# One more seven-product group a layer; copies of the weight sums moved to ScalarE; input sums queued behind the last split

## The chip, the cores and the metric

The kernel runs on one core of a Trainium2 chip. A core has TensorE (matmuls; the profile calls it PE, its weight loads PEld), VectorE (DVE), ScalarE (ACT), GpSimd (POOL) and SyncE (SP). Each engine works through its own queue in order. Transfers can be issued from SP, ScalarE and GpSimd, and an issue is one entry in that queue. The metric is the device time of one execution in microseconds; less is better.

## What is computed

A decoder of two layers on one sequence of 512 tokens of width 1024. Cut to what matters here:

```
for l in range(2):
    h = rms_norm(x, norm_mix[l])
    (m_qk, m_v, m_o, m_i, m_f, r_x, r_g, a_q, a_k, a_v, a_qi, a_ki, a_w, gates) = split(h @ w_in[l])
    ... three branches: mLSTM, RG-LRU, sparse attention ...
    x = x + merged @ w_out[l]
    h = rms_norm(x, norm_ffn[l])
    ff_g, ff_u = split(h @ ffn_up[l])                 # 3072 columns each
    ff_g = causal_dwconv(ff_g, ffn_conv_w[l], ffn_conv_b[l])
    x = x + (gelu(ff_g) * ff_u) @ ffn_down[l]
out = rms_norm(x, norm_final)
```

All of it is in float32.

## The kernel before, in words

**Units and splits.** The weights are packed into units of 128 x 1024 floats (512 KB) in the order of their use. SP loads a unit into a `raw` buffer (two of them; during seven-product groups two `quad` buffers more). ScalarE then writes its high part `wh` and VectorE the rest `wl` (`hl_split`, lines 216 and 217), up to three or four units ahead of their use. The inputs are kept the same way as `xh` and `xl`. A product is three matmuls: `wl` with `xh`, `wh` with `xl`, `wh` with `xh`.

**Sections of a layer.** `mv` (line 306), then `sm`, `rx`, `qk`, `qi`, `q`, `k`, `av`, `mo` (lines 262 and 268), with the mLSTM, the recurrence, the index scores and the attention as streams that are advanced between the groups; then the merged branches and the output projection, the second norm, and the feed-forward part in three chunks of eight columns of 128. `rope_pair` sends its results through DRAM with transfers from GpSimd. `k_turn`, `gd` and `g` are steps of the first sections; `g` (line 773) is loaded by GpSimd for the mLSTM. Each norm raises `rs` to the power -0.5 on GpSimd (lines 376 and 399). In layer 0 the rope tables are made on VectorE beside `mv` and `sm`.

**Seven-product groups.** Two feed-forward columns take four plain groups (`f_group`, 24 matmuls of 512 columns each). Pairs that stand in `QUADS` are made by seven products of half the size instead of eight (`quads`, `q_mm`, line 296: 24 matmuls of 256 columns each). Such a group needs sums of input halves (`x_sums`, lines 1030 and 1033: four additions, four differences and four splits, once a layer) and sums of weight units. For each group `u` the weight sums are four DRAM tiles `wsb`, `wsc`, `wse`, `wsg`. Each is a copy of a unit and then an accumulating transfer that adds another unit or another sum: `wse` gets `wsc` added, and `wsg` gets `wse`.

**What sets the order.** The program is traced in one order, and a scheduler with a simulated time line decides in which order each engine's queue gets its entries. `tick` counts slots; at some slots it takes the next step of `g_sums` (line 142). Copies and additions are all issued from GpSimd. Nothing in the program ties them to an instruction of another engine, except that an addition waits for its copy and for the sum that it adds. `tc.issue_after(ins)` (here `after`) queues what it encloses behind `ins` on that instruction's engine; it is an order of issue, not a wait for its end.

Of the kernel before, what the change touches and what calls it, by code (L numbers as in the profile page):

```python
# [15 lines left out]
ALU = mybir.AluOpType  # L16
# [20 lines left out]
NK = 385  # L37


QUADS = {(0, 4), (0, 6)} | {(c, i) for c in (1, 2) for i in (0, 2, 4, 6)}  # L40
SECTIONS = ("mv", "sm", "rx", "qk", "qi", "q", "k", "av", "mo")


# [1 line left out]
def tile_trunk(ctx, tc, x, pos, wts, chan, rgw, const, norm_mix, norm_ffn, norm_final, out, depth=2, dbg=None):  # L45
    nc = tc.nc
    V, A, T, G = nc.vector, nc.scalar, nc.tensor, nc.gpsimd

    def pool(name, bufs, **kw):
        return ctx.enter_context(tc.tile_pool(name=name, bufs=bufs, **kw))  # L50
# [4 lines left out]
    slot = pool("slot", 1)  # L55
# [21 lines left out]
    def S1(tag, shape=(P, 4, 512), dt=F32):  # L77
        return slot.tile(list(shape), dt, tag=tag, name=tag)
# [35 lines left out]
    for l in range(depth):  # L114
        u = l * per
        ffn = u + per - (NH // HC) * 3 * HC
        plan += [(u + i, None) for i in range(ffn - u)]
        u = ffn
        for c in range(NH // HC):
            for g in range(HC // 2):  # L120
                if (c, 2 * g) in QUADS:
                    plan += [(u, o) for o in "abcedfg"]
# [6 lines left out]
    st = dict(dma=0, spl=0, use=0, slot=0)  # L129
    raws, spl, alt, own = {}, {}, {}, {}  # L130
    wsum = {}
# [8 lines left out]
            extra.add(i)  # L140

    def g_sums():
        def put(dst, src, **kw):
            G.dma_start(out=dst, in_=src, max_dma_last_dim=1024, **kw)

        def first_(u):
            w = wsum[u]
            for k, n in (("b", 0), ("c", 1), ("e", 0), ("g", 3)):
                yield put(w[k], wts[u + n])

        def then(u):
            w = wsum[u]
            for k, src in (("b", wts[u + 1]), ("c", wts[u + 2]), ("e", w["c"]), ("g", w["e"])):
                yield put(w[k], src, accum_op=ALU.add)

        gs = list(wsum)
        yield from first_(gs[0])
        for u, v in zip(gs, gs[1:] + [None]):
            f = first_(v) if v is not None else iter(())
            for _ in then(u):  # L160
                yield 1
                yield next(f, None)

    bg = g_sums()

    def held(l):
# [48 lines left out]
    def hl_split(ps, h, l):  # L215
        a = A.activation(out=h, in_=ps, func=AF.Copy)  # L216
        v = V.tensor_tensor(out=l, in0=ps, in1=h.bitcast(F32), op=ALU.subtract)  # L217
        return a, v

    def after(ins):  # L220
        return tc.issue_after(getattr(ins, "ins", ins))
# [2 lines left out]

    def tick():
        st["slot"] += 1
        p = st["slot"] % 308
        if p > 8 and p % (3 if p < 170 else 2 if p < 220 else 4) == 0:
            next(bg, None)

    def pump():
        tick()
        for g in list(streams):
            if g[1]:
                with tc.high_priority():
                    r = next(g[0], None)
            else:
                r = next(g[0], None)
            if r is None:
                streams.remove(g)  # L240
# [47 lines left out]
    def q_mm(ps, x, start=True):  # L288
        tick()
        h, l = [w.rearrange("p (k c) -> p k c", c=2 * P) for w in unit()]  # L290
        for j in (1, 0):
            i = 0
            for k in range(4):
                for a, b in ((l, 0), (h, 1), (h, 0)):
                    i += 1
                    T.matmul(ps[:, j * 256:(j + 1) * 256], lhsT=a[:, k, j * P:(j + 1) * P], rhs=x[b][:, k, :],  # L296
                             start=start and j == 1 and i == 1, stop=j == 0 and i == 12,
                             skip_group_check=True)
# [205 lines left out]
    for l in range(depth):  # L504
        if l == 0:
            res["src"] = x
            nrm = Norm(norm_mix[0:1, :], ("S1", "S2", "S4", "S5"))
# [7 lines left out]
            v = nrm.scaled(0)  # L515
# [7 lines left out]
            with after(st["pair"][0]), after(st["pair"][1]):  # L523
                v = nrm.scaled(1)
# [7 lines left out]
                with after(a1[1]):  # L532
                    v = nrm.scaled(2)
# [3 lines left out]
                    v = nrm.scaled(3)  # L537
# [8 lines left out]
        e = SimpleNamespace()  # L546
# [471 lines left out]
        nrm = Norm(norm_ffn[l:l + 1, :], ("S9", "S6"))  # L1018
# [7 lines left out]
        def x_sums():  # L1026
            qa, qb = [S1(g, (P, 2, 4, 256)) for g in ("S6", "S9")]
            a = [qa[:, 0], qa[:, 1], qb[:, 0], qb[:, 1]]
            for n in (2, 3, 0, 1):
                V.tensor_tensor(out=a[n], in0=xq[n][0].bitcast(F32), in1=xq[n][1].bitcast(F32), op=ALU.add)  # L1030
            for key, g, d, i0, i1, op in (("b", "S1", 3, 2, 3, ALU.subtract), ("c", "S2", 2, 0, 2, ALU.subtract),
                                          ("e", "S3", 0, 3, 0, ALU.subtract), ("f", "S7", 1, 1, 0, ALU.add)):
                V.tensor_tensor(out=a[d], in0=a[i0], in1=a[i1], op=op)
                o = S1(g, (P, 2, 4, 256), dt=FR)
                hl_split(a[d], o[:, 0], o[:, 1])
                xq[key] = (o[:, 0], o[:, 1])
# [41 lines left out]
            for j in range(2):  # L1078
                hidden(i + j, m + j, gt[:, j, :], up[j])

        x_sums()
        nch = NH // HC
        for cidx in range(nch):
            hh = [S1("S4", dt=FR), S1("S6", dt=FR)]
            hl = [S1("S5", dt=FR), S1("S9", dt=FR)]
            i = 0
            while i < HC:
                m = cidx * HC + i
                if (cidx, i) in QUADS:
                    quads(i, m)  # L1090
# [12 lines left out]
            if end:  # L1103
                nrm = Norm(norm_final[0:1, :] if last else norm_mix[l + 1:l + 2, :], ("S1", "S2"))
# [19 lines left out]
def _pack(w_in, w_branch, w_out, ffn_up, ffn_down, depth):  # L1124
# [10 lines left out]
    for l in range(depth):  # L1135
# [41 lines left out]
        for c in range(NH // HC):  # L1177
            for i in range(0, HC, 2):
                m = c * HC + i
                if (c, i) in QUADS:  # L1180
                    for k, o in ((0, 0), (0, DFF), (D // 2, DFF), (D // 2, 0)):
# [82 lines left out]
```

## Time and profile before

| | |
|---|---|
| Median of three runs | 2179.81 us (2177.36 to 2180.73) |
| Profiled execution | 2172.2 us, of which its span is 2170.4 us |
| Busy, share of the span | TensorE 88%, VectorE 58%, ScalarE 40%, GpSimd 10% |
| Software queue of GpSimd's transfers | 127.44 MB, 24.7% of 16 engines |
| Queue of SP's loads | 200.30 MB, 29.2% of 16 engines |
| Chain that ended last | PE 81%, DMA 14%, DVE 3% |

The page cuts the span into 40 slices of 54 us and gives the busy share of each engine in tenths; for the granted TensorE clock and the share of the transfer engines there are rows of the same kind. A group's row gives line, engine, operation, tiles, count, then busy time and mean, then the idle time ahead of it and what ended it. A row of the timeline is start, length, engine, line, operation, tiles, with the idle time ahead of it in square brackets.

### The profile page before, as it was taken

What the parts mean: (1) busy time and instruction counts of PE and PEld (TensorE: products, weight loads), DVE (VectorE), ACT (ScalarE), POOL (GpSimd) and SP (SyncE); (2) the same over time, 40 slices, a digit from 0 to 9 for tenths busy, and PEclk for the clock granted to TensorE, in tenths of its full rate; (3) what the DMA queues carried; (4) which work ended last, traced back from release to release, by engine and by line L of the source; (5) the groups of instructions that cost most, each with busy time, mean ns of one, the idle gap of its engine ahead of it and who ended that gap; (6) DMA issues with size and microseconds to landing.
All of it is one profiled execution on the core that took longest, in us unless ns stands there. A gap on an engine that the chain in (4) does not pass through costs nothing.

```text
span 2170.4 us, 26601 instructions
## 1 busy us (share of the span) xinstructions
PE 1909.3 (88%) x10380; PEld 1627.7 (75%) x10380; DVE 1265.5 (58%) x2131; ACT 863.1 (40%) x1309; POOL 223.1 (10%) x314
## 2 busy tenths in 40 slices
PE   2366006999999999999999999999999999999998
PEld 1244004888888888989899878888888788999896
DVE  1252006786864447647667579777834457667584
ACT  1133004444444235425345466444342334445353
POOL 3433432121000000000000101210000000000000
PEclk6678557999999999999999999999999999999999
DMA  9999999675232332435454325853232233455452
GB/s 324 280 288 283 218 202 233 187 212 144 78 100 93 94 110 94 154 109 185 136 163 145 135 88 154 240 155 93 69 121 87 90 114 126 137 157 165 132 175 82
DMA packets 121758, 333.74 MB, mean 154 GB/s; under 512 B 10904, under 2 KB 52376, under 8 KB 119584
## 3 DMA queue, kind: packets, MB, share of 16 engines
q1 hardware_dynamic: 55584, 200.30, 29.2%
q0 software_dynamic: 64320, 127.44, 24.7%
q10 hardware_dynamic: 1728, 4.31, 0.6%
q8 instruction: 81, 1.33, 0.3%
q14 instruction: 45, 0.37, 0.1%
HBM read 312.06 MB, written 103.30 MB: 191 GB/s over the span
## 4 chain that ended last, share of the span: by engine, by line
PE 81%; DMA 14%; DVE 3%; issue 1%; ACT 1%; POOL 0%; POOLq 0%; ACTq 0%; DVEq 0%
PE A L262 25%; PE A L306 19%; PE A L268 12%; PE s L296 11%; PE t L296 5%; DMA wsc<-in_wts_dram 5%; DMA wsb<-in_wts_dram 5%; PE o L296 2%; DMA wse<-wsc 2%; PE o L836 1%; DMA wse<-in_wts_dram 1%; DMA wsg<-in_wts_dram 1%; PE o L762 1%; PE s L797 1%; PE t L849 1%
## 5 line engine op out<-in xcount | busy, mean ns | idle before, releaser
L262 PE MATMUL A<-xh,wl 128*128 128x512 f32 (+1 forms) x1072 | 428.5, 402 | 158.8 <-DVE wl L217 157.7
L217 DVE TENSOR_TENSOR wl<-raw,wh 128x1024 fp32r<-128x1024 f32 x294 | 358.8, 1222 | 350.2 <-ACT wh L216 348.1
L262 PE MATMUL A<-xl,wh 128*128 128x512 f32 (+1 forms) x1072 | 424.4, 398 | 4.2 <-DVE xl L217 4.2
L216 ACT ACTIVATE wh<-raw 128x1024 fp32r<-128x1024 f32 x294 | 309.8, 1056 | 296.7 <-PE A L306 127.5
L262 PEld LDWEIGHTS A<-xh,wl 128*128 128x128 f32 x1072 | 207.0, 193 | 213.7 <-DVE wl L217 154.8
L268 PE MATMUL A<-xh,wh 128*128 128x512 f32 (+1 forms) x1072 | 275.5, 391 | 0.0
L306 PE MATMUL A<-wh,S 128*128 128x512 f32 x832 | 256.1, 390 | 0.0
L262 PEld LDWEIGHTS A<-xl,wh 128*128 128x128 f32 x1072 | 207.2, 193 | 50.3 <-DVE xl L217 4.9
L268 PEld LDWEIGHTS A<-xh,wh 128*128 128x128 f32 x1072 | 195.5, 188 | 43.0 <-issue 0.5
L306 PEld LDWEIGHTS A<-wh,S 128*128 128x128 f32 x832 | 156.3, 188 | 33.3
L306 PE MATMUL A<-wl,S 128*128 128x512 f32 x416 | 162.6, 394 | 0.0
L296 PE MATMUL s<-S,wh 128*128 128x256 f32 x768 | 138.8, 282 | 0.0
L296 PEld LDWEIGHTS s<-S,wh 128*128 128x128 f32 x768 | 118.8, 190 | 0.2
L296 PE MATMUL s<-S,wl 128*128 128x256 f32 x384 | 108.1, 282 | 0.0
L469 DVE SCALAR_TENSOR_TENSOR m<-A,ch,m 128x511 f32<-128x511 f32 (+2 forms) x88 | 64.8, 744 | 46.1 <-ACT m L465 45.2
L306 PEld LDWEIGHTS A<-wl,S 128*128 128x128 f32 x416 | 78.1, 188 | 16.4
L399 POOL TENSOR_TENSOR rs<-rs,half 128x1 f32<-128x1 f32 x16 | 8.9, 557 | 743.8 <-DVE rs L398 730.7
L417 PE MATMUL s<-kst,xn 128*128 128x128 f32 x128 | 19.6, 301 | 72.1 <-DVE xn L383 72.1
L788 DVE TENSOR_TENSOR dmb<-g,kst 128x128 f32<-128x128 f32 x32 | 8.9, 285 | 116.1 <-DMA g<-gd 115.0
L262 PE MATMUL A<-S,wl 128*128 128x512 f32 x192 | 75.6, 395 | 0.5 <-ACT S L687 0.5
L262 PE MATMUL A<-S,wh 128*128 128x512 f32 x192 | 75.1, 393 | 0.0
L296 PEld LDWEIGHTS s<-S,wl 128*128 128x128 f32 x384 | 73.0, 190 | 0.2
(292 smaller groups left out, 3569.3 us busy)
## 6 DMA issues: line engine op xcount, KB each, us to landing
raw<-in_wts_dram SPq DMA_DIRECT2D x266, 512.0 KB, 3.6
wsb<-in_wts_dram POOLq DMA_DIRECT2D x40, 512.0 KB, 16.6
wsc<-in_wts_dram POOLq DMA_DIRECT2D x40, 512.0 KB, 16.9
quad<-in_wts_dram SPq DMA_DIRECT2D x28, 512.0 KB, 3.7
wse<-in_wts_dram POOLq DMA_DIRECT2D x20, 512.0 KB, 15.3
wsg<-in_wts_dram POOLq DMA_DIRECT2D x20, 512.0 KB, 15.7
wse<-wsc POOLq DMA_DIRECT2D x20, 512.0 KB, 18.3
wsg<-wse POOLq DMA_DIRECT2D x20, 512.0 KB, 21.5
```

The costliest lines, as they stand in the source:

```text
L216: a = A.activation(out=h, in_=ps, func=AF.Copy)
L217: v = V.tensor_tensor(out=l, in0=ps, in1=h.bitcast(F32), op=ALU.subtract)
L262: T.matmul(ps, lhsT=a[:, k, :], rhs=b[:, k, :], start=(i == 0), stop=False)
L268: T.matmul(ps, lhsT=wh[:, k, :], rhs=b_h[:, k, :], start=False, stop=(i == n))
L296: T.matmul(ps[:, j * 256:(j + 1) * 256], lhsT=a[:, k, j * P:(j + 1) * P], rhs=x[b][:, k, :], start=start and j == 1 and i == 1, stop=j == ...
L306: T.matmul(ps, lhsT=a[k0 + j][:, tt], rhs=b[:, j, :], start=(start and i == 1), stop=(stop and i == n))
L417: ins = T.transpose(ps[:, c * P:(c + 1) * P], xn[:, k * P:(k + 1) * P], ident)
L469: V.scalar_tensor_tensor(out=acc[:, d:], in0=ps[:, :S - d], scalar=ch[:, cw + j * step:cw + j * step + 1], in1=acc[:, d:], op0=ALU.mult, o ...
L762: T.matmul(po[:, 0:129], lhsT=SD[:, sb * P:(sb + 1) * P], rhs=e.mv[:, sb, h, :], start=(sb == 0), stop=(sb == tb))
L797: T.matmul(ps[:, sb * P:(sb + 1) * P], lhsT=e.qkF[1][:, h, sb * P:(sb + 1) * P], rhs=e.qkF[0][:, h, ts], start=True, stop=True)
L836: T.matmul(po[:, h * 64:(h + 1) * 64], lhsT=pc[:, c * P:(c + 1) * P], rhs=e.av[:, c, h * 64:(h + 1) * 64], start=(c == 0), stop=(c == t))
L849: T.transpose(pp[:, c * P:(c + 1) * P], pt[c // (t + 1)][:, c % (t + 1) * P:(c % (t + 1) + 1) * P], ident)
```

## The change

There are three edits. `QUADS` gets the pair (0, 2), so each layer has eleven seven-product groups for ten, and four sums more. In `g_sums` a step is now one copy, issued from ScalarE, and the addition of the step before, issued from GpSimd; the copies of a group follow in the order b, c, e, g, without a burst for the first group. `tick` takes a step at every fifth slot (after the first 14 of 308) and queues the copy on ScalarE behind the last weight split that was traced. `x_sums` is traced inside `after(nrm.last[1])`, so that its work on VectorE is queued behind the last `xl` split of the norm.

```diff
-QUADS = {(0, 4), (0, 6)} | {(c, i) for c in (1, 2) for i in (0, 2, 4, 6)}
+QUADS = {(0, 2), (0, 4), (0, 6)} | {(c, i) for c in (1, 2) for i in (0, 2, 4, 6)}
...
     def g_sums():
-        def put(dst, src, **kw):
-            G.dma_start(out=dst, in_=src, max_dma_last_dim=1024, **kw)
-
-        def first_(u):
-            w = wsum[u]
-            for k, n in (("b", 0), ("c", 1), ("e", 0), ("g", 3)):
-                yield put(w[k], wts[u + n])
-
-        def then(u):
-            w = wsum[u]
-            for k, src in (("b", wts[u + 1]), ("c", wts[u + 2]), ("e", w["c"]), ("g", w["e"])):
-                yield put(w[k], src, accum_op=ALU.add)
-
-        gs = list(wsum)
-        yield from first_(gs[0])
-        for u, v in zip(gs, gs[1:] + [None]):
-            f = first_(v) if v is not None else iter(())
-            for _ in then(u):
+        late = []
+        for u, w in wsum.items():
+            for k, n, m in (("b", 0, wts[u + 1]), ("c", 1, wts[u + 2]), ("e", 0, w["c"]), ("g", 3, w["e"])):
+                nc.scalar.dma_start(out=w[k], in_=wts[u + n], max_dma_last_dim=1024)
+                late.append((w[k], m))
+                if len(late) > 1:
+                    dst, src = late.pop(0)
+                    G.dma_start(out=dst, in_=src, max_dma_last_dim=1024, accum_op=ALU.add)
                 yield 1
-                yield next(f, None)
+        dst, src = late.pop(0)
+        G.dma_start(out=dst, in_=src, max_dma_last_dim=1024, accum_op=ALU.add)
+        yield 1
...
     def tick():
         st["slot"] += 1
-        p = st["slot"] % 308
-        if p > 8 and p % (3 if p < 170 else 2 if p < 220 else 4) == 0:
-            next(bg, None)
+        if st["slot"] % 308 > 14 and st["slot"] % 5 == 0:
+            with after(st["pair"][0]):
+                next(bg, None)
...
-        x_sums()
+        with after(nrm.last[1]):
+            x_sums()
```

How this moves instructions is seen at three places. The line numbers of the changed kernel are 8 lower from `tick` on (7 behind `x_sums`).

The first place is the start of the program on GpSimd. `rs` is the norm's power, `ws` tiles are the weight sums (the number behind the letter is the unit of the group), `cs` the rope tables, `gd` what `g` is loaded from. Before:

```order
L144 DMA wsb93_152<-in_wts_dram 512x256
L144 DMA wsc93_153<-in_wts_dram 512x256
L144 DMA wse93_154<-in_wts_dram 512x256
L144 DMA wsg93_155<-in_wts_dram 512x256
L144 DMA wsb97_156<-in_wts_dram 512x256
```

Eleven more of this kind follow, then the first power, and after it most of the other sums. Now:

```order
L368 TENSOR_TENSOR rs_252<-rs_252,half_95 128x1
L368 TENSOR_TENSOR rs_273<-rs_273,half_95 128x1
L368 TENSOR_TENSOR rs_290<-rs_290,half_95 128x1
L368 TENSOR_TENSOR rs_321<-rs_321,half_95 128x1
L452 DMA cs_515<-sinT_94 128x512
L452 DMA cs_515<-cosT_93 128x512
L566 DMA S10_550<-cs_515 32x2x512 x2
L150 DMA wsb89_152<-in_wts_dram 512x256
L150 DMA wsc89_153<-in_wts_dram 512x256
L606 DMA gd_587<-S9_559 4x512
L765 DMA g3_1212<-gd_587 128x512
```

The four powers and the tables come first, and two additions stand ahead of `gd` and `g` where before there were more than a hundred transfers.

The second place is section `rx` of layer 0 on ScalarE: `m1` is the first step of the convolution, `S4` and `S5` are the gates that follow a matmul of the convolved group, `wh` is a weight split. Before:

```order
L465 ACTIVATE m1_639<-A_612,ch_277 128x512
L885 ACTIVATE S4_603<-s_663,ch_277 128x512
L889 ACTIVATE S5_604<-s_678,bx_598 128x512
L216 ACTIVATE wh_510<-raw_423 128x1024
L465 ACTIVATE m1_682<-A_650,ch_277 128x512
L885 ACTIVATE S4_603<-s_707,ch_277 128x512
```

Now:

```order
L457 ACTIVATE m1_645<-A_619,ch_285 128x512
L208 ACTIVATE wh_650<-raw_522 128x1024
L588 ACT_TABLE_LOAD
L588 ACTIVATE g3_562<-g3_562 4x512
L457 ACTIVATE m1_688<-A_656,ch_285 128x512
L208 ACTIVATE wh_693<-raw_617 128x1024
L146 DMA wsb89_152<-in_wts_dram 512x256
L457 ACTIVATE m1_732<-A_699,ch_285 128x512
```

The splits have moved ahead of the gates, and the first copy of a weight sum stands behind one of them.

The third place is the second norm of layer 0. On GpSimd, the norm's powers `rs` of its four token tiles before:

```order
L1004 DMA S11_4217<-in_x_dram 128x2x1024
L399 TENSOR_TENSOR rs_4835<-rs_4835,half_95 128x1
L399 TENSOR_TENSOR rs_4887<-rs_4887,half_95 128x1
L399 TENSOR_TENSOR rs_4942<-rs_4942,half_95 128x1
L399 TENSOR_TENSOR rs_4998<-rs_4998,half_95 128x1
```

Now:

```order
L150 DMA wsc133_181<-in_wts_dram 512x256
L150 DMA wse133_182<-wsc133_181 512x256
L391 TENSOR_TENSOR rs_4850<-rs_4850,half_95 128x1
L391 TENSOR_TENSOR rs_4903<-rs_4903,half_95 128x1
L391 TENSOR_TENSOR rs_4958<-rs_4958,half_95 128x1
L150 DMA wsg133_183<-wse133_182 512x256
L391 TENSOR_TENSOR rs_5013<-rs_5013,half_95 128x1
```

Three additions now stand among the powers. On VectorE, at the end of that norm, before (`xl` are the last splits of the norm, `S6` and `S9` the input sums, `wx` the split of a weight unit):

```order
L401 SCALAR_TENSOR_TENSOR xn_4996<-S12_4218,rs_4998,grow_4665 128x512
L1030 TENSOR_TENSOR S6_5022<-xh_90,xl_91 128x1024 x2
L217 TENSOR_TENSOR xl_91<-s_5007,xh_90 128x4x128
L217 TENSOR_TENSOR xl_91<-s_5014,xh_90 128x4x128
L217 TENSOR_TENSOR wx_5295<-quad_5294,wx_5295 128x1024
L1030 TENSOR_TENSOR S9_5023<-xh_90,xl_91 128x1024 x2
```

Now:

```order
L393 SCALAR_TENSOR_TENSOR xn_5011<-S12_4232,rs_5013,grow_4679 128x512
L209 TENSOR_TENSOR xl_91<-s_5022,xh_90 128x4x128
L209 TENSOR_TENSOR xl_91<-s_5029,xh_90 128x4x128
L1022 TENSOR_TENSOR S6_5038<-xh_90,xl_91 128x1024 x2
L1022 TENSOR_TENSOR S9_5039<-xh_90,xl_91 128x1024 x2
L209 TENSOR_TENSOR wx_5081<-quad_5080,wx_5081 128x1024
```

The two last splits have moved ahead of the first input sums.

## The prediction

> **What bounds the kernel now.** I read the page's slices first, then its chain and its list of transfers.
>
> ```profile
> span 2170.4 us, 26601 instructions
> PE 1909.3 (88%) x10380; PEld 1627.7 (75%) x10380; DVE 1265.5 (58%) x2131; ACT 863.1 (40%) x1309; POOL 223.1 (10%) x314
> PE   2366006999999999999999999999999999999998
> PEclk6678557999999999999999999999999999999999
> DMA  9999999675232332435454325853232233455452
> wsb<-in_wts_dram POOLq DMA_DIRECT2D x40, 512.0 KB, 16.6
> ```
>
> There are two regimes. From slice 8 on (54 us each) TensorE is full and at full clock, so there only TensorE's own work counts. In the seven slices before it is mostly idle and the DMA row is full. The windows and the waits of that stretch say who fills it:
>
> ```profile
> 240.00:300.00 60.00, 0.00 (x0) 0.00 (x0) 0.00 (x0) 0.00 (x0) 24.82 (x26) 0.50 1.23 201
> ...
> 410.00:440.00 30.00, 30.00 (x150) 24.99 (x149) 22.93 (x48) 12.73 (x24) 9.18 (x17) 1.00 0.90 272
> ...
> 1370.00:1400.00 30.00, 30.00 (x157) 25.30 (x156) 23.71 (x51) 12.81 (x26) 7.05 (x13) 1.00 0.87 238
> ```
> ```profile
> PE A L262 <- DVE wl L217: 157.3, 7, 128.9
> PE s L417 <- DVE xn L383: 72.1, 3, 28.5
> ...
> ACT D L791 <- DVE dmb L788: 108.9, 1, 108.9
> ```
>
> In a windows row the columns after the length are the busy times of TensorE, its weight loads, VectorE, ScalarE and GpSimd, then clock, DMA share and GB/s. In 240 to 300 us no compute engine does anything while GpSimd issues 26 transfers. The timeline shows why everybody stands:
>
> ```profile
> 7.20 0.15 DVE L375 TENSOR_SCALAR rs<-rs 128x1 f32<-128x1 f32 x1
> 26.59 0.59 POOL L376 TENSOR_TENSOR rs<-rs,half 128x1 f32<-128x1 f32 x1
> 29.91 0.76 PE L306 MATMUL A<-wl,xh 128*128 128x512 f32 x1 [0.76 <-ACT xh L216]
> 307.71 0.61 POOL L773 DMA_DIRECT2D g<-gd  x1 [1.44 <-DMA wsc<-in_wts_dram]
> 356.52 1.01 POOL L144 DMA_DIRECT2D wsg<-wse  x1 [1.58 <-DMA wsg<-wse]
> 359.17 1.01 POOL L144 DMA_DIRECT2D wsg<-wse  x1 [1.64 <-DMA wsg<-wse]
> ```
>
> The 160 transfers of the weight sums (lines 144) sit in GpSimd's queue with nothing to hold them back, so they run at the start, one per 2.65 us at the end (356.52 to 359.17). The first norm's power is ready to go at 7.35 us and runs at 26.59; the reload of `g`, which the mLSTM, then ScalarE (108.9 us) and then the weight splits (128.9 us) wait for, gets its turn at 307.71. The bound of the opening is GpSimd's queue, not the arithmetic.
>
> **The opening.** Its cost without the sums is read from layer 1, whose same sections ran with no sums beside them:
>
> ```profile
> 631.34 0.72 POOL L1004 DMA_DIRECT2D S<-in_x_dram  x1 [82.22 <-PE s L862]
> 1571.99 0.71 POOL L1004 DMA_DIRECT2D S<-xs  x1 [77.52 <-PE s L862]
> ```
> ```profile
> 1223.19 0.39 PE L306 MATMUL A<-wl,xh 128*128 128x512 f32 x1
> ```
> ```profile
> 1247.56 3.73 PE A L262 x16
> ```
>
> The same step of the two layers lies 940.65 us apart: that is a full layer with TensorE dense. Section `mv` takes 1247.56 - 1223.19 = 24.4 us, and from there to the end are 2170.4 - 1247.56 = 922.8 us. The new GpSimd queue has the four powers first, so the first matmul comes at 7.35 + (29.91 - 26.59) = 10.7 us. The other three tiles of x then pass one after another through the same norm, and ScalarE and VectorE also make the rope tables there, which layer 1 does not: for what TensorE waits in this I bound 0 (layer 1's pace) and 40 (three more chains of about 9.3 us, 3.3 of them from power to matmul, and a 12 us wait for the positions), and take 12, nearer the low end since a block of twelve matmuls covers most of each chain. So the second section starts at 10.7 + 24.4 + 12 = 47.1, and the span would be 47.1 + 940.65 + 922.8 = 1910.6.
>
> **One more seven-product group a layer.**
>
> ```profile
> 877.83 3.73 PE A L262 x16
> ...
> 883.43 3.73 PE A L262 x16
> ...
> 889.03 2.88 PE t L296 x24
> ...
> 928.89 1.16 PE A L306 x5
> ```
>
> A plain group is 883.43 - 877.83 = 5.60 us, four are 22.4. The two seven-product groups of this chunk take (928.89 - 889.03)/2 = 19.9. One more in each layer saves 2 x 2.5 = 4.9 us. It also starts two columns earlier, while VectorE still makes the input sums:
>
> ```profile
> L217 DVE TENSOR_TENSOR wl<-raw,wh 128x1024 fp32r<-128x1024 f32 x294 | 358.8, 1222 | 350.2 <-ACT wh L216 348.1
> ```
>
> Behind the last norm split VectorE has, up to the weight split of the second product, some 13 passes of 128x1024 at 1.2 us and four short ones of 0.7: 19 to 20 us, to about 866. TensorE has the rest of its halves (to 850.5), two plain groups and the first product, to 864.6. So it waits about 2 us in each layer: 4 in all, bounds 0 (sums as well hidden as now) and 12.
>
> **Input sums behind the last split.** The timelines of VectorE and of TensorE, before:
>
> ```profile
> 844.89 2.36 DVE L1030 TENSOR_TENSOR S<-xh,xl 128x1024 f32<-128x1024 f32 x2 [2.95 <-PE s L417]
> 847.17 1.28 DVE L217 TENSOR_TENSOR xl<-s,xh 128x512 fp32r<-128x512 f32 x2
> ```
> ```profile
> 847.90 0.39 PE L262 MATMUL A<-xl,wh 128*128 128x256 f32 x1 [2.12 <-DVE xl L217]
> ...
> 848.84 0.35 PE L262 MATMUL A<-xh,wl 128*128 128x256 f32 x1
> ...
> 852.37 0.40 PE L262 MATMUL A<-xl,wh 128*128 128x512 f32 x1
> ```
>
> Two sums of 2.36 us stand ahead of the splits that TensorE waits for (2.12 us idle), and from 848.84 to 852.37 the matmuls run at half rate, which loses about 1.5 more. With the splits first both go: 3.6 in each layer, 7.2 in all. What is late next is the chain of the norm itself.
>
> The Trainium skill ("TensorE: Matmul & The Clock Gate", Part 1) has the clock halved only after an idle window of about 3.4 us. The row shows a slow stretch of 3.5 us behind a gap of 2.1, so here the measurement decides; by the rule the edit would give 4.2 instead of 7.2.
>
> **What the new issuing adds.** 88 copies leave from ScalarE and 88 additions from GpSimd.
>
> ```profile
> 0.74 0.40 ACTq L359 DMA_DIRECT2D grow<-in_norm_mix_dram  x1
> ```
> ```profile
> S<-dh POOLq DMA_DIRECT2D x16, 512.0 KB, 6.7
> ```
> ```profile
> 814.64 1.22 DVE L217 TENSOR_TENSOR wx<-raw,wx 128x1024 fp32r<-128x1024 f32 x1
> ```
> ```profile
> 822.59 0.57 POOL L399 TENSOR_TENSOR rs<-rs,half 128x1 f32<-128x1 f32 x1 [164.58 <-DVE rs L398]
> ...
> 840.59 0.55 POOL L399 TENSOR_TENSOR rs<-rs,half 128x1 f32<-128x1 f32 x1 [6.53 <-ACT xh L216]
> ```
>
> ScalarE's issue: 88 x 0.40 = 35 us at most exposed (92 if an issue takes the 1.05 of an addition on GpSimd); ScalarE is 40% busy and the splits are made three units ahead, so I take 1. An addition now waits in GpSimd's queue for its copy, and in layer 0's second norm the powers stand behind it. The copy of `wse133` goes out behind the split that ends at 814.6, and its addition also needs the one of `wsc133` landed: some 4 us for that copy and 6.7 for its addition (the nearest calm transfer of this size from GpSimd) make 825, so the power at 822.59 comes 3 us later, the one at 840.59 about 2, and one at the layer's end about 1: 6 in all, bounds 0 and 30 (with the 16.6 us of the crowded stretch, three times). Behind these powers stand ScalarE's scaling, the transposes and TensorE.
>
> Contention: the additions go at 2.65 us when nothing else runs; with a copy of some 2 us that is 4.7 us of transfer per step of five slots, 14 us, a third of what the engines can do. Where the share is 0.3 to 0.5 that is free. Where it is 0.90 and 0.87 (the rope's transfers) the sum reaches the 1.23 of the crowded rows. There loads landed as this row of the loads to 400 us says, and TensorE's pace was as in the two below:
>
> ```profile
> DMA to landing us min/median/max: 3.6/7.7/12.2
> ```
> ```profile
> 158.83 0.50 PE L262 MATMUL A<-xh,wl 128*128 128x512 f32 x1 [2.98 <-DVE wl L217]
> ...
> 176.18 0.56 PE L262 MATMUL A<-xh,wl 128*128 128x512 f32 x1 [2.98 <-DVE wl L217]
> ```
>
> With two buffers 7.7 us still feeds a 5.6 us group. Bounds 0, and 53: if each load took 12.2 us and 2.3 of split, (14.5/2 - 5.6) = 1.65 us for each of some 32 units in the two rope stretches (90 us each). I take 6.
>
> **The sum.** 1910.6 - 4.9 + 4 - 7.2 + 1 + 6 + 6 = 1915.5 us of span. The profiled execution took 2172.2, 1.8 more than its span, so 1917.3. The median shown (2179.81) lies 7.6 above that execution; part of that will belong to the crowded opening. I add 3 and predict **1920**.
>
> **The rivals.**
> *The transfers collide (0.18).* The sums leave the opening but crowd the rope stretches and the loads for the seven-product groups: 1920 + 53, about 1970. For it: 0.90 + 0.33 is the crowded level. Against: TensorE never waited at 0.90. The Trainium skill ("DMA: Bandwidth & Descriptors", Issuing engines are not separate DMA queues) says that another issuing engine brings no bandwidth, only issue time; nothing in these rows speaks against it, and it is this rival's ground.
> *The opening stays slow (0.10), so that the change does not do what it says.* The groups of `rx` come 17.35 us apart (158.83 to 176.18) because the order of the program puts each split behind the gates of the group before; if that remains, four groups cost 4 x 11.75 = 47 more: about 1967. For it: the wait in these rows is on VectorE's split, not on a load. Against: the new order has the splits ahead of the gates.
> *ScalarE's queue is held (0.03): slower than before.* Most copies also wait in the built order for an earlier transfer on their semaphore, so one can stand until a load lands (3.6 at the quickest), with the next split behind it. 88 x 3.6 = 317 us give about 2237. It decides the sign once a copy costs TensorE more than (2180 - 1920)/88 = 2.95 us. Against: with splits three units ahead a hold of 3.6 us reaches TensorE only if several come together.
>
> **Chances.** The forecast with its own bounds (1893 to 1945) has 0.65, a still shorter time 0.04, the three rivals 0.31. The range 1893 to 1975 leaves out the shorter times, the third rival and the far tails. 0.2%, some 4 us, is what a measurement can tell. Faster 0.96, same 0.01, slower 0.03.
>
> **What would show it.** Right: no idle GpSimd-bound stretch before 60 us, section `sm` starting at 45 to 50, the first reload of `g` before 90, the same step of the two layers still about 940 apart, no wait of TensorE on the last `xl` split. Wrong: TensorE waiting for weight splits between 50 and 150 or in the rope stretches, powers late in the second norm by more than 5 us, or a wait of ScalarE ahead of its copies.

## The result and the profile after

The changed kernel takes 1924.32 us (median of 4 runs, 1917.29 to 1925.64), the kernel before 2178.59 us (2175.59 to 2180.73). The ratio is 0.8827, 95% interval 0.8802 to 0.8852. The forecast was 1920, range 1893 to 1975. One execution below, the profiled one of the run that leaves out the rope stretch alone, was disturbed (3084.22 us at a granted clock of 0.556), so that run is told by the times of its other four.

The page of the changed kernel, the rows that answer to those of before (slices are now 48 us):

```profile
span 1923.7 us, 27039 instructions
PE 1882.1 (98%) x10524; PEld 1617.5 (84%) x10524; DVE 1272.4 (66%) x2151; ACT 867.2 (45%) x1318; POOL 180.2 (9%) x242
PE   8998999999989999999999989999999999999998
PEclk9999999999999999999999999999999999999999
DMA  5577985556667878878754789756566545354442
wsb<-in_wts_dram ACTq DMA_DIRECT2D x22, 512.0 KB, 4.4
wsb<-in_wts_dram POOLq DMA_DIRECT2D x22, 512.0 KB, 7.2
```

TensorE is at least 80% busy in every slice, the granted clock is at least 0.9 in each, and the DMA row is spread over the program instead of standing at 9 for seven slices. In the last two rows, the first (ACTq) are the copies of `wsb`, the second (POOLq) its additions: an addition lands in 7.2 us, where copies and additions together took 16.6. GpSimd's timeline shows the two steps that the forecast named:

```profile
7.28 0.56 POOL L368 TENSOR_TENSOR rs<-rs,half 128x1 f32<-128x1 f32 x1 [6.83 <-DVE rs L367]
84.73 1.15 POOL L765 DMA_DIRECT2D g<-gd  x2 [5.17 <-DMA gd<-S]
```

The first power runs at 7.28 (26.59 before), the first reload of `g` at 84.73 (307.71 before). What TensorE still waits for, by its waits view (engine and line, what it waited for, total us, times, longest):

```profile
PE s L695 <- DMA S<-dl: 11.9, 2, 6.0
PE s L409 <- ACT xn L392: 6.0, 1, 6.0
...
PE s L789 <- DVE g L792: 3.2, 1, 3.2
...
PE t L288 <- ACT gate L1061: 1.4, 2, 0.7
```

The wait on the last `xl` split (4.2 in all before) is gone. New are two waits of 6 us on the rope's transfers (`S<-dl`), one of 6 us on a late power of the second norm (`xn`), and one of 3.2 in the rope stretch. (The rope stretch is where `rope_pair` sends its results through DRAM: it writes `dh` and `dl` and reads them back into `S`.) The start of section `sm` in each layer, and the last VectorE instruction of the changed kernel:

```profile
41.38 0.39 PE L254 MATMUL A<-xh,wl 128*128 128x512 f32 x1
...
997.07 0.40 PE L254 MATMUL A<-xh,wl 128*128 128x512 f32 x1
```
```profile
1919.14 0.75 DVE L393 SCALAR_TENSOR_TENSOR xn<-S,rs,grow 128x512 f32<-128x512 f32 x1 [0.73 <-POOL rs L391]
```

| Part of the span | forecast | measured |
|---|---|---|
| start to section `sm` | 47.1 | 41.4 |
| `sm` of layer 0 to `sm` of layer 1 | 946.1 | 955.7 |
| `sm` of layer 1 to the end of the span | 922.3 | 926.6 |
| span | 1915.5 | 1923.7 |

(The forecast's terms are split as it placed them: the powers' 6 in layer 0, the others half to each layer, so 940.65 + 5.45 and 922.8 - 0.55.) The end of the span lies 3.8 us behind the last VectorE instruction (1919.9) now and 6.3 before (2164.1); this remainder differs from kernel to kernel, so the runs below are compared by the end of that instruction, called "the end". It comes from one profiled execution of each kernel, and executions of one kernel differ (1917.29 to 1925.64 here), so a few us between two ends are not firm.

### The profile page after: what moved, and what is told of

Same layout as the page of the kernel before. It is cut to its first block, busy times and chain, and to the rows that moved or that the text cites. A ratio compares the mean times of both kernels' runs of the same rounds, so it can differ in the third digit from the quotient of the medians.

```text
span 1923.7 us, 27039 instructions
## 1 busy us (share of the span) xinstructions
PE 1882.1 (98%) x10524; PEld 1617.5 (84%) x10524; DVE 1272.4 (66%) x2151; ACT 867.2 (45%) x1318; POOL 180.2 (9%) x242
## 4 chain that ended last, share of the span: by engine, by line
PE 83%; DMA 7%; DVE 5%; ACT 2%; issue 1%; POOL 1%; ACTq 0%; SPq 0%; POOLq 0%; DVEq 0%
PE A L254 22%; PE A L298 21%; PE s L288 13%; PE A L260 11%; PE t L288 6%; PE o L288 3%; DVE wl L209 2%; PE o L828 2%; DMA dl<-m 2%; DMA raw<-in_wts_dram 1%; DMA dh<-th 1%; DVE m L461 1%; PE t L841 1%; DMA wsc<-in_wts_dram 1%; ACT wh L208 1%
## 5 line engine op out<-in xcount | busy, mean ns | idle before, releaser
L254 PE MATMUL A<-xh,wl 128*128 128x512 f32 (+1 forms) x1008 | 395.9, 395 | 3.7 <-DVE m L461 2.1
L254 PE MATMUL A<-xl,wh 128*128 128x512 f32 (+1 forms) x1008 | 392.7, 392 | 0.0
L260 PE MATMUL A<-xh,wh 128*128 128x512 f32 (+1 forms) x1008 | 262.0, 392 | 0.0
L254 PEld LDWEIGHTS A<-xh,wl 128*128 128x128 f32 x1008 | 190.2, 189 | 48.8 <-DVE wl L209 4.0
L254 PEld LDWEIGHTS A<-xl,wh 128*128 128x128 f32 x1008 | 190.4, 189 | 42.5 <-issue 2.2
L260 PEld LDWEIGHTS A<-xh,wh 128*128 128x128 f32 x1008 | 182.8, 188 | 39.9 <-issue 1.2
L934 ACT ACTIVATE th<-A 128x512 f32<-128x512 f32 x48 | 28.6, 596 | 104.2 <-PE A L260 76.6
L288 PE MATMUL t<-xh,wl 128*128 128x256 f32 x256 | 72.1, 282 | 0.7 <-ACT gate L1061 0.7
L843 ACT ACTIVATE g<-t 128x512 f32<-128x512 f32 (+2 forms) x48 | 25.2, 524 | 105.0 <-PE t L841 104.6
L288 PE MATMUL t<-xl,wh 128*128 128x256 f32 x256 | 72.3, 282 | 0.0
```

The lines of the kernel that those rows point to most:

```text
L254: T.matmul(ps, lhsT=a[:, k, :], rhs=b[:, k, :], start=(i == 0), stop=False)
L260: T.matmul(ps, lhsT=wh[:, k, :], rhs=b_h[:, k, :], start=False, stop=(i == n))
L843: A.activation(out=pT[:, :n * P], in_=pp[:, :n * P], func=AF.Copy)
L934: A.activation(out=th, in_=pg, func=AF.Tanh, scale=0.5)
```

## The experiments

### Which edit ended the slow opening

**Copies issued from GpSimd again**, all else as changed:

```diff
-                nc.scalar.dma_start(out=w[k], in_=wts[u + n], max_dma_last_dim=1024)
+                G.dma_start(out=w[k], in_=wts[u + n], max_dma_last_dim=1024)
```

> The changed kernel with the copies issued from GpSimd again; pace of the steps, eleven groups and the input sums' place as changed. The steps are traced as far apart as in the changed kernel, but nothing binds a copy to an instruction of GpSimd, and in the built order the copies stand at the head of its queue, 16 of them ahead of the first power. Theory of the forecast (the opening is bound by what stands ahead in GpSimd's queue): as slow as before the change, 2130 to 2200, first power behind 20 us, g's reload behind 250 us. Rival (the pace of the steps is what helps, and the issuing engine doesn't matter): 1920 to 1930.

Measured: 2192.86 us, ratio to before 1.0069 (1.0045 to 1.0094). The page's TensorE slices and GpSimd's timeline:

```profile
PE   2366002999999999999999999999999999999998
```
```profile
27.14 0.59 POOL L368 TENSOR_TENSOR rs<-rs,half 128x1 f32<-128x1 f32 x1
...
339.25 0.61 POOL L765 DMA_DIRECT2D g<-gd  x1 [1.69 <-DMA wsg<-wse]
```

The empty slices are back, the first power runs at 27.14 and `g` at 339.25. Tracing the steps further apart does nothing by itself: in GpSimd's queue nothing holds a copy back.

**Copies from ScalarE, not bound to a split**:

```diff
-            with after(st["pair"][0]):
-                next(bg, None)
+            next(bg, None)
```

> The changed kernel with its copies still issued from ScalarE but not bound behind a split. In the built order nine copies then stand ahead of ScalarE's second weight split, nearly all 88 within its first hundred entries, and the additions follow at the head of GpSimd's queue, with three of them ahead of gd's reload's place for each one now. Theory that binding (pace on the chip) is what ends the slow opening: the transfers crowd the first 300 us again, first g reload behind 200 us, 2100 to 2190. Rival, that taking half of the sums off GpSimd's queue is enough: 1920 to 1980.

Measured: 2214.66 us, ratio 1.0171 (1.0146 to 1.0197): slower than either range. Slices of the page, two rows of ScalarE's timeline (ACTq is its queue, the length of such a row the time that the issue takes), and one of GpSimd's:

```profile
PE   3310441899999999999999999999999999999998
```
```profile
50.93 9.17 ACTq L146 DMA_DIRECT2D wsb<-in_wts_dram  x1
...
72.97 0.60 ACT L208 ACTIVATE xh<-s 128x512 fp32r<-128x512 f32 x1 [21.48 <-issue]
```
```profile
335.61 0.61 POOL L764 DMA_DIRECT2D g<-gd  x1 [1.42 <-DMA wsc<-in_wts_dram]
```

So the engine alone does not help either. All 88 copies go out in the first 222 us, and an issue takes up to 9.17 us; behind four issues in a row ScalarE's next split starts 21.48 us after the end of the split before. The additions then fill GpSimd's queue again, and the reload of `g` comes at 335.61. The first part is the forecast's third rival, ScalarE's queue held and the kernel slower than before, though here the issues themselves are long, where the rival had copies waiting for an earlier transfer. With the binding, none of this is seen.

**Copies from SyncE, bound behind a load**:

```diff
-                nc.scalar.dma_start(out=w[k], in_=wts[u + n], max_dma_last_dim=1024)
+                nc.sync.dma_start(out=w[k], in_=wts[u + n], max_dma_last_dim=1024)
...
-            nc.sync.dma_start(out=r[1], in_=src)
+            st["load"] = nc.sync.dma_start(out=r[1], in_=src)
...
-            with after(st["pair"][0]):
+            with after(st["load"]):
                 next(bg, None)
```

> The changed kernel with the copies issued from SyncE, each bound behind the load of a weight unit that was traced last, in place of ScalarE and a split. Theory that the binding counts and the engine does not: opening as in the changed kernel (section sm at 41 to 43 us), 1915 to 1935. Rival, that ScalarE matters (a copy in SyncE's queue that waits for an earlier transfer holds the weight loads behind it): TensorE waits for splits or loads at many places, over 1950.

Measured: 1942.81 us (1939.16 to 1943.30), between the two ranges. The opening is that of the changed kernel (section `sm` at 41.38). What is lost comes later:

```profile
PE t L676 <- DVE S L811: 13.8, 2, 8.0
```
```profile
254.35 1.06 POOL L150 DMA_DIRECT2D wse<-wsc  x1 [14.28 <-DMA wse<-in_wts_dram]
255.04 1.45 POOL L809 TENSOR_TENSOR rp<-rs,half 128x4 f32<-128x4 f32 x1
```

The second fence is GpSimd's timeline: the engine stands 14.28 us until the copy for the addition at the head of its queue has landed, the power `rp` behind it, and TensorE waits 8.0. With the binding the slow opening is gone on either of the two engines tried; where the additions then meet other work differs between the two.

### What the sums still cost

**No sums**: the kernel leaves out copies and additions, and the seven-product groups load plain units.

```diff
-                nc.scalar.dma_start(out=w[k], in_=wts[u + n], max_dma_last_dim=1024)
-                ...
                 yield 1
...
-            src = wts[u] if op is None else wsum[u][op] if op in wsum[u] else wts[u + {"a": 0, "d": 3, "f": 2}[op]]
+            src = wts[u] if op is None else wts[u + {"a": 0, "b": 1, "c": 2, "d": 3, "e": 0, "f": 2, "g": 3}[op]]
```

> The changed kernel without the weight sums: neither copies nor additions run, and the seven-product groups load plain units in their place, so all matmuls, splits and loads stay and only the values differ. In the changed kernel's trace TensorE's gaps come to 6.0 (second norm), 5.9, 6.0 and 3.2 us (rope stretches), 2.1 (behind a convolution) and some smaller, and three of the long ones are followed by a half-clock stretch that loses about 1.6. If the sums cause all of these but the convolution's, the span falls by 6.0+5.9+6.0+3.2 and 3 x 1.6 = 26 us, to 1898. If the gaps belong to the rope transfers and the norm themselves, the span stays at 1920 or above.

**Copies only**: the copies run, the additions are left out.

```diff
-                late.append((w[k], m))
-                if len(late) > 1:
-                    dst, src = late.pop(0)
-                    G.dma_start(out=dst, in_=src, max_dma_last_dim=1024, accum_op=ALU.add)
                 yield 1
```

> The changed kernel with its 88 copies from ScalarE but without the 88 additions from GpSimd (the summed units then hold copies). Queue theory: an addition that waits for its copy at the head of GpSimd's queue holds the rope's transfers and the norm's power behind it; without additions the gaps go, and the span is within 5 us of the kernel without sums (1898 to 1903). Transfer theory: what slows the rope is the share of the transfer engines that the sums take; the copies have about a third to a half of it, so half of the gain stays away: 1908 to 1914. It also prices the issue of the copies on ScalarE, forecast at 1 us.

Measured: 1904.44 us (1904.20 to 1904.95) without sums, 1906.70 (1906.02 to 1906.80) with copies only. Their last VectorE rows:

```profile
1892.37 0.75 DVE L385 SCALAR_TENSOR_TENSOR xn<-S,rs,grow 128x512 f32<-128x512 f32 x1 [0.73 <-POOL rs L383]
```
```profile
1893.43 0.75 DVE L386 SCALAR_TENSOR_TENSOR xn<-S,rs,grow 128x512 f32<-128x512 f32 x1 [0.73 <-POOL rs L384]
```

By the end, the sums cost 1919.9 - 1893.1 = 26.8 us (26 expected), the copies 1.1 of it, the additions 25.7. That is where the queue theory had it, but the run takes the additions' bytes away as well as their waits, so it does not yet tell the two apart. (In both kernels the span goes on for 10 us behind that row instead of 3.8, which hides 6 us of the gain in their times; why was not found.)

**Additions traced two steps behind their copies**:

```diff
-                if len(late) > 1:
+                if len(late) > 2:
```

> The changed kernel with each addition issued two steps (28 us) behind its copy instead of one step. Same transfers, same bytes. Queue theory: by then every copy has landed (the slowest took about 12 us), so an addition no longer waits in GpSimd's queue; the 6.0 us gap in the second norm goes, and those of the rope stretches shrink: 1900 to 1910. Transfer theory: unchanged, 1920 to 1926, with the rope's gaps as before.

Measured: 1919.14 us (1913.82 to 1921.62), end 1916.0. GpSimd's timeline at the second norm, in the changed kernel and in this one:

```profile
565.10 1.01 POOL L150 DMA_DIRECT2D wsc<-in_wts_dram  x1 [11.24 <-DMA wsc<-in_wts_dram]
575.04 1.01 POOL L150 DMA_DIRECT2D wse<-wsc  x1 [8.93 <-DMA wsc<-in_wts_dram]
575.69 0.97 POOL L391 TENSOR_TENSOR rs<-rs,half 128x1 f32<-128x1 f32 x1
```
```profile
576.68 1.01 POOL L150 DMA_DIRECT2D wse<-wsc  x1 [8.19 <-DMA wsc<-in_wts_dram]
577.33 0.98 POOL L391 TENSOR_TENSOR rs<-rs,half 128x1 f32<-128x1 f32 x1
```

Both show the chain: an addition waits for the one before it to land (which in the first row waited for its copy), and the power stands behind. In the changed kernel it was ready at 569.90 and runs at 575.69. But the edit did not do what was meant: nothing ties an addition in GpSimd's queue, and the scheduler puts it where its copy should be done, however late it is traced. The run tells the theories apart no better than before.

**Additions held back on GpSimd**, two steps behind their copies:

```diff
+        def add(dst, src):
+            z = sml.tile([P, 4, 2], F32, tag="ba", name="z")
+            op = G.tensor_tensor(out=z[:, 0, 0:1], in0=st["low"][:, 0:1].bitcast(F32), in1=half[:, 0:1], op=ALU.add)
+            with after(op):
+                G.dma_start(out=dst, in_=src, max_dma_last_dim=1024, accum_op=ALU.add)
...
-                if len(late) > 1:
-                    dst, src = late.pop(0)
-                    G.dma_start(out=dst, in_=src, max_dma_last_dim=1024, accum_op=ALU.add)
+                if len(late) > 2:
+                    add(*late.pop(0))
...
+            st["low"] = l
```

> The changed kernel with each addition two steps behind its copy, and held there: GpSimd first adds one column of the newest split's low part to a constant (a 128x1 operation whose result nobody reads), and the addition's transfer is queued behind that. In the run with additions merely traced later, their rows on GpSimd did not move. Same transfers and bytes as the changed kernel, five additions still fall into each rope stretch. Queue theory (an addition waits at the head of GpSimd's queue for its copy or the addition before it, and the rope's transfers or the power wait behind it): the copies have landed long before, the waits of 7 to 12 us ahead of the additions go, TensorE's gaps of 5.9, 3.2, 6.0 and 6.0 us shrink below 1 us each, and the last VectorE instruction ends at 1895 to 1900 (1919.9 in the changed kernel, 1893.1 without sums). Transfer theory (the bytes of the sums slow the rope's transfers): the power's gap of 6.0 goes, the three of the rope stretches stay at 3 us or more, and the end is at 1910 to 1915.

Measured: 1917.06 us (1916.84 to 1918.93), end 1911.4. The gaps at the power (6.0), of 3.2 and of 6.0 in the rope stretches are gone or below 1.2; the first of the rope stays. TensorE's timeline there:

```profile
164.57 0.55 PE L701 MATMUL s<-ki,S 128*128 128x256 f32 x1 [4.47 <-DMA dh<-th]
```

How long the twelve rope writes `dh` of layer 0 take to land (least, median, most), in the changed kernel, in this one and without sums:

```profile
DMA to landing us min/median/max: 4.5/8.5/14.2
```
```profile
DMA to landing us min/median/max: 4.3/5.3/9.1
```
```profile
DMA to landing us min/median/max: 2.8/3.7/4.9
```

Neither theory holds alone. The late power belongs to the queue: with the additions held back its gap goes. For the rope, the changed kernel's own trace says more than this run. GpSimd's rows ahead of the gap of 3.2, in layer 0, then a row of GpSimd and the one of TensorE at the gap of 6.0, in layer 1:

```profile
191.07 1.08 POOL L150 DMA_DIRECT2D wsg<-wse  x1 [10.84 <-DMA wsg<-in_wts_dram]
191.74 0.95 POOL L494 DMA_DIRECT2D S<-dh  x1
...
192.79 1.00 POOL L490 DMA_DIRECT2D dh<-th  x1
```
```profile
1106.97 0.53 POOL L494 DMA_DIRECT2D S<-dl  x1 [0.67 <-DMA dl<-m]
...
1118.07 0.55 PE L695 MATMUL s<-ki,S 128*128 128x256 f32 x1 [6.00 <-DMA S<-dl]
```

In layer 0 an addition waits 10.84 us, and the rope's transfers leave in one burst behind it; this `dh` lands only 14.2 us after its issue, and VectorE waits 7.7 for it. In layer 1 no addition stands ahead: `S<-dl` goes out 0.67 us after the entry before it, and takes 11.0 us to land, against 7.7 in the kernel without sums. So that gap, like the 4.5 that stays here, goes with slow landings and not with a wait in the queue. Whether the landings are slow because of the bytes on the transfer engines, or because additions and rope share GpSimd's queue of transfers, no run tells apart; the copies alone, which go through ScalarE's queue, move the median landing of `dh` only from 3.7 to 4.3 us. The end is where the transfer theory had it, but the instrument has a price too: its operation reads a split, so that split's buffer comes free later, GpSimd waits for that split (up to 9.9 us just ahead of the rope stretch), and small new waits of TensorE appear. How the 18.2 us above the kernel without sums divide between bytes, order and instrument stays open.

**No steps in the rope stretch and around the second norm**:

```diff
-        if st["slot"] % 308 > 14 and st["slot"] % 5 == 0:
+        p = st["slot"] % 308
+        if p > 14 and p % 5 == 0 and not (36 < p < 64 or 150 < p < 172):
```

> The changed kernel that takes no step of the sums in the rope stretch (slots 37 to 63 of a layer) nor around the second norm (slots 151 to 171); the steps left out there come later, so all sums are still made. Both theories: gaps of the rope and the norm go, 1898 to 1905. If the sums then come too late for the last groups of layer 0 (46 steps are wanted by slot 290, 48 are taken), TensorE waits there for a load of a sum, and the span is above 1915.

**No steps in the rope stretch alone** (the same line without `or 150 < p < 172`):

> The changed kernel that takes no step of the sums in the rope stretch (slots 37 to 63 of a layer) but does around the second norm. The run without steps at either place ended at 1890.8 (last VectorE instruction), the changed kernel at 1919.9, 29.1 apart; in the changed kernel's trace the late power shows a gap of 6.0 and a half-clock stretch that loses 1.6. If that is its price, this run ends at 1898 to 1900 with a gap in the second norm, and 21 of the 29 belong to the rope; if steps shift so that no addition is under way at the power, it ends at 1891.

Measured: 1897.12 us (1896.40 to 1902.55; ratio 0.8713, 0.8697 to 0.8729) without steps at both places, the fastest of all. All sums are still made. TensorE's largest waits there (total, times, longest):

```profile
PE A L299 <- DVE wl L209: 2.7, 3, 1.2
PE A L255 <- DVE m L462: 2.1, 1, 2.1
```

No gap of the power is left, none of the rope above 0.7 us, and the end is 1890.8, 29.1 us before the changed kernel's. Without steps in the rope stretch alone the median is 1906.86 (1905.15 to 1907.70): the steps around the second norm cost 9.7 us by these medians (7.6 was expected from the gap and its half clock), the rope stretch the other 17 to 19. So the sums are nearly free where they meet nothing that GpSimd must do in time: this end is even 2.3 us before that of the kernel without sums, a difference for which no cause was found.

### Sizes of the other terms

Both on the kernel without steps at the two places, since it has the fewest other gaps. **Ten groups**:

```diff
-QUADS = {(0, 2), (0, 4), (0, 6)} | {(c, i) for c in (1, 2) for i in (0, 2, 4, 6)}
+QUADS = {(0, 4), (0, 6)} | {(c, i) for c in (1, 2) for i in (0, 2, 4, 6)}
```

> The kernel that takes no steps in the rope stretch and around the second norm, with ten seven-product groups a layer as before the change. The eleventh group was forecast to save 2.5 us a layer and to cost a stall of 2 us a layer: by that sum 1 us more than with eleven. The stall is not in the trace with eleven groups, so the newer expectation is the full 4.9 us: end of the last VectorE instruction at 1895.7 instead of 1890.8. Rival: the group is limited by VectorE's input sums, and ten are as fast (within 1 us).

Measured: 1903.82 us (1902.69 to 1908.00), 6.7 more. Other gaps moved as well (the end is 11.7 later, in the longest of the five executions), so the group's own worth is read from the feed-forward part: last power of the second norm to first power of the next norm, on GpSimd. With eleven groups, then with ten (layer 0, then layer 1):

```profile
576.75 0.55 POOL L392 TENSOR_TENSOR rs<-rs,half 128x1 f32<-128x1 f32 x1 [6.53 <-ACT xh L208]
939.15 0.56 POOL L392 TENSOR_TENSOR rs<-rs,half 128x1 f32<-128x1 f32 x1 [0.45 <-DVE rs L391]
...
1511.99 0.55 POOL L392 TENSOR_TENSOR rs<-rs,half 128x1 f32<-128x1 f32 x1 [6.53 <-ACT xh L208]
1874.45 0.56 POOL L392 TENSOR_TENSOR rs<-rs,half 128x1 f32<-128x1 f32 x1 [156.43 <-DVE rs L391]
```
```profile
578.16 0.55 POOL L392 TENSOR_TENSOR rs<-rs,half 128x1 f32<-128x1 f32 x1 [6.54 <-ACT xh L208]
943.64 0.56 POOL L392 TENSOR_TENSOR rs<-rs,half 128x1 f32<-128x1 f32 x1 [0.45 <-DVE rs L391]
...
1522.15 0.55 POOL L392 TENSOR_TENSOR rs<-rs,half 128x1 f32<-128x1 f32 x1 [6.53 <-ACT xh L208]
1886.18 0.56 POOL L392 TENSOR_TENSOR rs<-rs,half 128x1 f32<-128x1 f32 x1 [266.44 <-DVE rs L391]
```

362.40 and 362.46 with eleven, 365.48 and 364.03 with ten: 3.1 and 1.6, so 4.7 us in two layers. TensorE waits less than 1 us in each of the four stretches.

**Input sums not bound behind the last split**:

```diff
-        with after(nrm.last[1]):
-            x_sums()
+        x_sums()
```

> The same kernel (eleven groups, no steps in the rope stretch and around the second norm) with the input sums queued as before the change, not behind the last split of the norm. By the forecast's term each layer gets a gap of 2.1 us and a half-clock stretch that loses 1.5 back: 7.2 us more, the last VectorE instruction at 1898. By the clock rule (a gap of 2.1 us does not lower the clock) 4.2 more, 1895. If VectorE's work before the split is the same in total and only moves, no change.

Measured: 1906.79 us (1902.86 to 1907.74), 9.7 more; end 1897.2, 6.4 later, in the shortest of the five executions. The same gap comes in both layers, but only one is followed by a slow clock (TensorE's timeline, then windows of 2 us within 3 us of each gap; clock is the third figure from the right):

```profile
585.10 0.38 PE L255 MATMUL A<-xl,wh 128*128 128x256 f32 x1 [2.12 <-DVE xl L209]
...
1522.13 0.58 PE L255 MATMUL A<-xl,wh 128*128 128x256 f32 x1 [2.12 <-DVE xl L209]
```
```profile
586.00:588.00 2.00, 2.00 (x15) 1.87 (x14) 2.00 (x3) 0.00 (x0) 0.00 (x0) 1.00 0.26 35
...
1522.00:1524.00 2.00, 1.87 (x8) 1.87 (x9) 2.00 (x4) 0.34 (x1) 0.00 (x0) 0.50 0.00 0
```

The feed-forward parts, measured as above (577.78 to 942.30 and 1514.82 to 1880.88), are 2.1 us longer in layer 0 and 3.6 in layer 1: 5.7 together. The trace of the kernel before has the same two outcomes, the other way round: layer 0's gap is followed by the slow stretch that the forecast shows, layer 1's is not (TensorE's timeline, then a window behind the gap):

```profile
1788.53 0.39 PE L262 MATMUL A<-xl,wh 128*128 128x256 f32 x1 [2.12 <-DVE xl L217]
```
```profile
1790.00:1792.00 2.00, 2.00 (x13) 1.72 (x13) 2.00 (x3) 0.00 (x0) 0.00 (x0) 1.00 0.32 57
```

**Twelve groups**, with a step at every fourth slot:

```diff
-QUADS = {(0, 2), (0, 4), (0, 6)} | {(c, i) for c in (1, 2) for i in (0, 2, 4, 6)}
+QUADS = {(0, 0), (0, 2), (0, 4), (0, 6)} | {(c, i) for c in (1, 2) for i in (0, 2, 4, 6)}
...
-        if p > 14 and p % 5 == 0 and not (36 < p < 64 or 150 < p < 172):
+        if p > 14 and p % 4 == 0 and not (36 < p < 64 or 150 < p < 172):
```

> The kernel without steps in the rope stretch and around the second norm, with the pair (0, 0) too (twelve seven-product groups a layer) and a step at every fourth slot, so that the 96 sums are ready in time. The run with ten groups showed that a group is worth 2.3 us a layer, which gives 4.6 less: the last VectorE instruction at 1886 and about 1892 in time. Against it stands the term of the forecast that the eleventh group did not show: the first product now follows the norm at once, and VectorE's input sums, 19 us of work, then stand ahead of TensorE. If they are late by more than 2.3 us a layer the kernel is no faster than with eleven (1897).

Measured: 1941.26 us (1936.62 to 1945.23). TensorE's timeline at the first product of layer 0 (layer 1 has the same 8.22):

```profile
593.68 0.58 PE L289 MATMUL t<-xh,wl 128*128 128x256 f32 x1 [8.22 <-DVE wl L209]
```

The stall on VectorE that the forecast feared for the eleventh group is real for the twelfth: 8.2 us a layer for a group worth 2.3. The run changes two things, and the rest of its 44 us is not divided between them; one more gap, 4.9 us at a power of layer 1's first norm, stands behind an addition.

## Why the prediction was right, point by point

**The bound and the opening: right, shown.** GpSimd's queue held the opening: with the copies back in it the old time returns; bound to ScalarE's or SyncE's work the copies leave it alone. First power and `g` came where the forecast had them (7.28 for 7.35; 84.73 for "before 90"). The three later chains of the first norm and the rope tables cost 41.4 - 10.7 - 24.4 = 6.3 us instead of the 12 that were taken, nearer still to layer 1's pace.

**The full layer of 940.65: near.** It comes from a stretch without sums. In the kernel without sums the two sections `sm` start 978.98 - 42.04 = 936.9 us apart, where the forecast's layer less its gains gives 940.65 - 2.45 - 3.6 = 934.6. In the changed kernel they are 955.7 apart, and the difference is what the sums cost.

**Eleventh group: right.** 4.7 us against 4.9. Its stall (4 taken, bounds 0 to 12) did not come: TensorE has no wait on VectorE there. The two waits of 0.7 on `gate` are in layer 1, on ScalarE's copy of a product, and the kernel without sums has four of them. The forecast's count gave TensorE 16.1 us of work (848.45 to 864.6) from the end of the last norm split to the end of the first product. In the changed kernel that split ends at 601.65 and the first product at 620.73, 19.1 us on (its row in the chain that ended last):

```profile
617.85 2.88 PE t L288 x24
```

So it was TensorE's cover that was undercounted, by 3 us, more than the 2 us of stall. With no plain group ahead the stall is 8.2.

**Input sums: right mechanism, size off.** 5.7 against 7.2. The forecast took the slow stretch of layer 0 for both layers; the trace before already had layer 1's gap without one, and 3.6 + 2.1 read from it would have been the 5.7 measured. The same gap is followed by a half clock in some cases only. The Trainium skill ("TensorE: Matmul & The Clock Gate", Part 1) says that the window over which activity is watched runs freely, and that the moment of the change depends on where in the window the first matmul lands. The two outcomes of one gap of 2.12 us agree with that; that the window's phase is their cause is not shown. The 3.4 us of idleness that the Trainium skill has there were not needed here: the half clock at 1522.13 comes with a gap of 2.12.

**ScalarE's issue: right.** 1 forecast, 1.1 between copies only and no sums.

**Powers and contention: the terms that were too small.** 6 for late powers, 6 for contention and 1 for the issue make 13; the sums cost 26.8. The mechanism of the powers was right (6.0 in one gap, and its half clock, against 3 + 2 + 1 in several), the norm's part by the two skipping runs 9.7. The step on contention priced late weight loads, for which TensorE hardly waited (4.0 us in all, 3.9 without sums). What the sums slowed are the rope's own transfers, for which TensorE waits soon after: some stand behind an addition that waits for its copy, and they land later than without sums (median of `dh` 8.5 us against 3.7). This term should have had what stands behind each addition in GpSimd's queue, and the landing of the rope's transfers beside one.

**The errors cancelled.** The forecast was 13.8 too small in the sums, 1.5 in the input sums and 0.2 in the eleventh group; it was 5.7 too large in the opening and 4 in the stall, and the end of the program took 2.5 less than before, which no term had. Together that is 3.3 of the 8.2 us between 1915.5 and 1923.7; the rest, the waits on `gate` among it, is not assigned. In time the 8.2 became 4.3, since 3 had been added for a median above the profiled execution, and here the median lies 1.2 below it. So the change and its main cause were foreseen; that 1920 came so near is luck.

**The forecast's own signs.** The opening, the reload of `g` and the wait on the last `xl` split came as under "right". Section `sm` starts at 41.4, earlier than its 45 to 50, and the same step of the two layers (377.78 and 1329.29) lies 951.5 apart and not about 940. One sign of "wrong" appeared: the power of the second norm ran 5.8 us after it was ready, where the forecast had put the limit at 5.

**The rivals.** Transfers collide: in part; what the sums cost beyond the forecast is 13.8 us instead of 53, waits in GpSimd's queue included. The opening stays slow: no; from 60 to 120 us TensorE is busy 59.9 of 60 us. ScalarE's queue held: not with the binding, yes without it.

## What to carry to other kernels

Work for an idle queue is not free because the queue is idle: see what will stand ahead of it at the start, and what behind each of its entries that waits. To pace it, bind it to an instruction in the queue that issues it; tracing it later moves nothing that a scheduler may hoist. Then leave out the stretches in which the same queue carries something urgent: here that was worth another 27 us. Ask too how late the urgent transfers land beside it, not only what stands ahead of them.

## What the runs showed of the hardware

An issue of a transfer from ScalarE takes 0.5 us when the transfers keep up, and up to 9.17 when 88 of them are sent within 222 us, with the engine's other work behind it. The Trainium skill ("DMA: Bandwidth & Descriptors", Issuing engines are not separate DMA queues) has the issue time as usually small beside the transfer. The bound copies agree (0.5 us, and 4.4 until `wsb` lands); of the unbound ones the longest issue does not (9.17, where the median copy lands after 11.8). The other surprise is the one gap of 2.12 us with and without a half clock behind it, in the same kernel.
